# Mixture-of-experts stage of a diffusion layer: extra tokens' input products moved to pieces 13 and 14, with branch hints for TensorE

## The chip, the core and the metric

The kernel runs on one core of one Trainium2 chip. The metric is the device time of one execution in microseconds. Before the change it is 2446.74 us, the median of 3 runs (2444.03 to 2450.15).

## What is computed

One layer of a diffusion generator on 1024 latent tokens of width 1024: modulated RMSNorm, one projection, two kinds of attention, an output projection, and then a mixture of experts, which is what the change touches. Each token goes to 4 of 32 experts:

```python
def expert_block(args):
    xb, e = args
    hcat = xb @ w_in[e] + b_in[e]
    x_glu = jnp.minimum(hcat[:, :D_FF], SWIGLU_LIMIT)
    x_lin = jnp.clip(hcat[:, D_FF:], -SWIGLU_LIMIT, SWIGLU_LIMIT)
    act = x_glu * jax.nn.sigmoid(SWIGLU_ALPHA * x_glu) * (x_lin + 1)
    return act @ w_out[e] + b_out[e]
```

`w_in[e]` is 1024 x 2048 and `w_out[e]` 1024 x 1024, both float32. The outputs are weighted by the router's gates and summed per token. How many tokens an expert gets is known only at run time; on average it is 128.

## The kernel before, in words

The experts are `stage_e`. Its outer loop makes one pass for each expert e, plus one at the end. A pass has two halves: 16 input pieces of expert e (`in_mm`, half a row block of `w_in` each), then 8 output pieces of expert e - 1 (`out_mm`). A piece is six matmuls of 128 x 512 for TensorE: weights are split into a high and a low part and three products are summed (`mm3`, L87 to L89). The split of a piece is one copy on ScalarE (`wh`, L1131) and one subtraction on VectorE (`wl`, L1132). `split_ahead` keeps it up to 5 pieces ahead of TensorE, into 5 buffers of each (`NW`): after piece i of a pass stands the split of piece i + 5, so that behind input piece 14 comes the split of output piece 3, and behind input piece 15 that of output piece 4.

The first 128 tokens of an expert are handled with every piece. Tokens beyond 128 (up to 64 of them, in two units of 32) are the extra tokens: `left_in` and `left_out` compute their products on TensorE alone, inside a branch on the expert's count (`beyond`, L1159 for the first unit, L1161 for the second). The count is read into a register of TensorE's sequencer by `value_load` (L1168). Where the branch is not entered, TensorE's sequencer waits at it until TensorE is done, and signals in place of the products.

The order of all engines' work is written out by hand (`manual_schedule`): each engine runs its instructions in the order of the program text, and waits where its data are not there. Around the change it is, for a pass:

- after input piece 11 (`LB`): two PSUM banks for the extra tokens are cleared by ScalarE (`blank`, L1104);
- after input piece 15: `act_a(e)` clamps the 128 tokens' sums from PSUM, on VectorE (`ga` L1195, `ln` L1197) with ScalarE's activation between (L1196); then `left_in(e)`; then SP's loads of the next expert's `w_in`; then `act_l(e)`, which does for the extra tokens what `act_a` does: four clamps on VectorE (`gal` L1204 and `lnl` L1205 for each unit), then ScalarE's activation (L1206);
- after output pieces 1, 3 and 4: `columns(e + 1, 0..2)`, which transposes the next expert's gathered tokens on TensorE (L1119) and brings them back with a copy on ScalarE (L1122 or L1125) and, for the first two, a subtraction on VectorE (L1123). The third is for the extra tokens and has no subtraction;
- after output piece 5 (`KB`): one PSUM bank is cleared for the extra tokens' outputs; after output piece 7, `left_out(e - 1)`.

The PSUM banks of `columns`, `act_cols` (the transposes of the activations), `blank` and `left_in` all come from one tag, "r", which has two buffers taken in turn. In a pass nine tiles take them: three of `act_cols`, the two extra-token banks, three of `columns`, and the bank of the extra tokens' outputs. A tile can be written when all readers of the tile two turns before it are done.

```python
            def ring():
                return ps.tile([128, 512], F32, name="r", tag="r", bufs=2)
```

GpSimd issues the gathers of the tokens (L1060, L1068) and the scatters of the results (L1278, L1283); SP issues the weight loads.

Of the kernel before, what the change touches and what calls it, by code (L numbers as in the profile page):

```python
# [48 lines left out]
class K:  # L49
# [963 lines left out]
    def stage_e(self):  # L1013
        nc, I, tc = self.nc, self.I, self.tc
        ep = self.ep
        win, wout = I["w_in"], I["w_out"]
        NE = 32
        with ExitStack() as ctx:
# [4 lines left out]
            VAL = {}  # L1023
# [74 lines left out]
            def ring():  # L1098
                return ps.tile([128, 512], F32, name="r", tag="r", bufs=2)

            def blank():

                p = ring()
                nc.scalar.activation(p, zero.to_broadcast([128, 512]), AF.Copy)  # L1104
                return p
# [48 lines left out]
                    self.mm3(H[e][:, 1024 * h + 512 * b:1024 * h + 512 * b + 512], xh[:, k, :], xlo[:, k, :],  # L1154
                             wh[:, c], wl[:, c], False, k == 7)

            def beyond(e, unit):

                with tc.If(VAL[e] > 128):  # L1159
                    unit(0)  # L1160
                    with tc.If(VAL[e] > 160):  # L1161
                        unit(1)

            def left_in(e):

                xc = XT[e][2]
                ls = L[e]
                VAL[e] = nc.tensor.value_load(self.cnt[0:1, e:e + 1], min_val=0, max_val=1024)  # L1168

                def unit(u):  # L1170
                    for f in range(4):
                        o = ls[u][32 * f:32 * f + 32, :]
                        for g in range(2):
                            c = 1024 * g + 256 * f
                            q, c = divmod(c, 1536)
                            nc.tensor.matmul(o[:, 256 * g:256 * g + 256], sel(e, q, 32).bitcast(F32),
                                             self.bias[:, c:c + 256].bitcast(F32), start=g == 0, stop=False,
                                             tile_position=(0, 32 * f))
                    for k in range(8):
                        j, h = divmod(k, 2)  # L1180
                        for f in range(4):
                            w = RAW_IN[e][k].rearrange("p (g c) -> p g c", g=2)[:, :, 256 * f:256 * f + 256]
                            nc.tensor.matmul(ls[u][32 * f:32 * f + 32, :],
                                             xc[:, 2 * u + h, 32 * j:32 * j + 32], w,
                                             start=False, stop=k == 7, tile_position=(0, 32 * f))

                beyond(e, unit)

            A, AL = {}, {}
            COLS, KB, ACI, RI, LB, KAB = (1, 3, 4), 5, (3, 5, 7), 1, 11, 6  # L1190

            def act_a(e):
                gm = sp.tile([128, D], F32, name="ga", tag="ga", bufs=1)
# [6 lines left out]
            def act_l(e):  # L1200
                gm = sp.tile([128, 2, 256], F32, name="gal", tag="gal", bufs=1)
                ln = sp.tile([128, 2, 256], F32, name="lnl", tag="lnl", bufs=1)
                for u in range(2):
                    nc.vector.tensor_scalar(gm[:, u], L[e][u][:, :256], 7.0, None, op0=OP.min)  # L1204
                    nc.vector.tensor_scalar(ln[:, u], L[e][u][:, 256:], 7.0, -7.0, op0=OP.min, op1=OP.max)  # L1205
                nc.scalar.activation(gm, gm, AF.Gelu_apprx_sigmoid)  # L1206
                AL[e] = [gm, ln]
# [7 lines left out]
            def act_cols(e, g):  # L1215
                gm, gl = A[e][0], AL[e][0]
                if g == 0:
                    x = self.ap.tile([128, 16, 128], F32R, name="at", tag="kSa" if e < NE - 1 else "Q0")
                    ACT[e] = (x[:, 0:8], x[:, 8:16],
                              sp.tile([128, 4, 128], F32, name="ac", tag="ac", bufs=1))  # L1220
                ah, al, ac = ACT[e]
                p = ring()
                for i in range(4):
                    src = gm[:, 512 * g + 128 * i:512 * g + 128 * i + 128] if g < 2 else \
                        gl[:, i // 2, 128 * (i % 2):128 * (i % 2) + 128]
                    nc.tensor.transpose(p[:, 128 * i:128 * i + 128], src, self.ident)
                p3 = p.rearrange("p (k q) -> p k q", k=4)
                if g < 2:
                    nc.scalar.activation(ah[:, 4 * g:4 * g + 4], p3, AF.Copy)
                    nc.vector.tensor_sub(al[:, 4 * g:4 * g + 4], p3, ah[:, 4 * g:4 * g + 4].bitcast(F32))  # L1230
                else:
                    nc.scalar.activation(ac, p3, AF.Copy)
                    A.pop(e)
# [13 lines left out]
            def left_out(e):  # L1247
                ac = ACT[e][2]
                p = Y[e][2]

                def unit(u):
                    for j in range(4):
                        nc.tensor.matmul(p[32 * j:32 * j + 32, 256 * u:256 * u + 256],
                                         sel(e, 1, 32).bitcast(F32),
                                         self.bias[:, 512 + 256 * j:768 + 256 * j].bitcast(F32),
                                         start=True, stop=False, tile_position=(0, 32 * j))
                    for k in range(8):
                        jj, h = divmod(k, 2)
                        for j in range(4):
                            nc.tensor.matmul(p[32 * j:32 * j + 32, 256 * u:256 * u + 256],  # L1260
                                             ac[:, 2 * u + h, 32 * jj:32 * jj + 32],
                                             RAW_OUT[e][k // 2][:, 1024 * (k % 2) + 256 * j:1024 * (k % 2) + 256 * j + 256],
                                             start=False, stop=k == 7, tile_position=(0, 32 * j))

                beyond(e, unit)

            def result(e):
                y0, y1, yl = Y.pop(e)
# [52 lines left out]
            for e in range(NE + 1):  # L1321
                if 0 < e < NE - 1:
                    gather(e + 1)
                for i in range(16 if e < NE else 0):
                    in_mm(e, i)
                    if e > 0 or i < 13:
                        split_ahead(1)
                    else:
                        done[1] += 1
                    if i == RI and e > 1:  # L1330
                        result(e - 2)
                    if i in ACI and e > 0:
                        act_cols(e - 1, ACI.index(i))
                    if i == 0 and e == 0:
                        LLS = left_lists()
                    if i == 2 and e == 0:
                        left_lists2(*LLS)
                        gather_left(0)
                        load_out(0, range(2, 4), nc.gpsimd)
                    if i in (9, 10) and e == 0:  # L1340
                        columns(1, i - 9)
                    if i == 11 and e == 0:
                        columns(0, 2)
                        gather_left(1)
                    if i == LB:
                        L[e] = [blank(), blank()]
                if e == NE:
                    result(e - 2)
                if e < NE:
                    act_a(e)  # L1350
                    left_in(e)
                if e + 1 < NE:
                    load_in(e + 1, range(8) if e else range(2, 8))
                if e == NE - 1:
                    load_out(e)
                if e == 0:
                    load_out(0, range(2))
                    act_l(0)
                    split_ahead()
                    columns(1, 2)  # L1360
                elif e < NE:
                    act_l(e)
                for k in range(8 if e > 0 else 0):
                    out_mm(e - 1, k)
                    split_ahead(1)
                    if e < NE:
                        if k in COLS and e + 1 < NE:
                            columns(e + 1, COLS.index(k))
                        if k == (KAB if e < NE - 1 else 3):
                            act_b(e)  # L1370
                        if e == NE - 1 and k in (5, 6, 7):
                            act_cols(e, (5, 6, 7).index(k))
                    if k == KB:
                        Y[e - 1].append(blank())
                if e == 0:
                    act_b(e)
                if e > 0:
                    left_out(e - 1)
                    if e < NE:
                        if e < NE - 1:  # L1380
                            load_out(e)
                        split_ahead()
# [168 lines left out]
```

## Time and profile before

| | |
|---|---|
| median of 3 runs | 2446.74 us |
| the profiled execution | 2445.95 us |
| its span, first to last instruction | 2444.2 us |
| experts' stage (weights of the first to the last) | about 937 to 2405 us |
| TensorE busy | 2275.3 us, 93% |
| VectorE busy | 1938.9 us, 79% |
| ScalarE busy | 1505.0 us, 62% |

PE is TensorE's matmuls, PEld its weight loads, PEq its sequencer, DVE is VectorE, ACT ScalarE, POOL GpSimd, SP SyncE. Busy times are unions of the recorded instructions; a matmul is drawn from its start to a modelled end, so that neighbours overlap. An instruction is named by its line in the kernel and by the tiles that it writes and reads (`out<-in`).

### The profile page before, as it was taken

The numbers are of one execution on the slowest core, as the hardware profiler recorded it, in microseconds if no ns is written. First come the engines' busy times: TensorE is split into PE (matmuls) and PEld (weight loads), VectorE is DVE, ScalarE is ACT, GpSimd is POOL, SyncE is SP. The second block draws the span as 40 slices with busy tenths as digits, with TensorE's granted clock in tenths as the row PEclk, the third lists the DMA queues.
The fourth block names the chain that finished last, engine by engine and source line by source line (L and its number), as shares of the span: only waits on it lengthen the run. The fifth ranks groups of instructions, "written<-read, shape, count | busy, mean of one in ns | idle before, by whom it ended". The sixth has DMA issues, their size and how long they took to land. (4 is left out here: it accounts for less than half of the span.)

```text
span 2444.2 us, 36800 instructions
## 1 busy us (share of the span) xinstructions
PE 2275.3 (93%) x13516; PEld 1760.8 (72%) x13516; DVE 1938.9 (79%) x3051; ACT 1505.0 (62%) x2285; POOL 549.3 (22%) x699
## 2 busy tenths in 40 slices
PE   6999999999999997989999999999999999999993
PEld 3787777787888775767667777767767777777762
DVE  5897087777998677988768898778878978887884
ACT  4321077777888324767656776666767766766762
POOL 2402100000344433122112222112212212222211
PEclk9999999999999997999999999999999999999996
DMA  7546141111110646889778898879779779787875
GB/s 266 182 142 198 48 141 36 35 27 44 30 24 18 231 162 241 326 339 330 263 265 334 306 350 316 292 266 370 279 279 384 285 296 355 281 321 299 311 272 173
DMA packets 133890, 557.00 MB, mean 228 GB/s; under 512 B 18720, under 2 KB 29632, under 8 KB 100880
## 3 DMA queue, kind: packets, MB, share of 16 engines
q1 hardware_dynamic: 103472, 476.21, 51.0%
q0 software_dynamic: 30176, 77.43, 11.4%
q8 instruction: 169, 2.77, 0.5%
q14 instruction: 73, 0.60, 0.1%
HBM read 495.04 MB, written 50.14 MB: 223 GB/s over the span
## 5 line engine op out<-in xcount | busy, mean ns | idle before, releaser
L1131 ACT ACTIVATE wh<-rin 128x1024 fp32r<-128x1024 f32 x520 | 550.3, 1060 | 251.4 <-PE H L89 218.8
L1132 DVE TENSOR_TENSOR wl<-rin,wh 128x1024 fp32r<-128x1024 f32 x520 | 619.4, 1219 | 102.2 <-ACT wh L1131 100.8
L87 PE MATMUL H<-wh,xt 128*128 128x512 f32 x1024 | 414.1, 404 | 0.6 <-issue 0.5
L88 PE MATMUL H<-wl,xt 128*128 128x512 f32 x1024 | 405.5, 396 | 0.6 <-DVE wl L1132 0.6
L89 PE MATMUL H<-wh,xt 128*128 128x512 f32 x1024 | 405.2, 396 | 0.0
L1132 DVE TENSOR_TENSOR wl<-rout,wh 128x1024 fp32r<-128x1024 f32 x248 | 296.5, 1222 | 88.4 <-ACT wh L1131 84.6
L1131 ACT ACTIVATE wh<-rout 128x1024 fp32r<-128x1024 f32 x248 | 256.7, 1054 | 47.1 <-PE H L89 27.2
L89 PEld LDWEIGHTS H<-wh,xt 128*128 128x128 f32 x1024 | 193.5, 189 | 45.7
L87 PEld LDWEIGHTS H<-wh,xt 128*128 128x128 f32 x1024 | 193.9, 189 | 43.5 <-issue 1.4
L88 PEld LDWEIGHTS H<-wl,xt 128*128 128x128 f32 x1024 | 194.0, 189 | 42.7 <-DVE wl L1132 1.0
L87 PE MATMUL y<-wh,at 128*128 128x512 f32 x512 | 210.8, 412 | 0.0
L88 PE MATMUL y<-wl,at 128*128 128x512 f32 x512 | 203.2, 397 | 0.5 <-DVE wl L1132 0.5
L89 PE MATMUL y<-wh,at 128*128 128x512 f32 x512 | 203.4, 397 | 0.0
L1060 POOL DMA_INDIRECT xg<-h2d,im x31 | 33.5, 1081 | 658.8 <-PE r L1119 658.2
L622 ACT ACTIVATE PT<-T 128x512 f32<-128x512 f32 (+1 forms) x256 | 140.8, 577 | 54.4 <-PE T L621 51.9
L1283 POOL DMA_INDIRECT acc<-ol,il x64 | 151.3, 2364 | 17.0 <-DVE wl L1132 15.2
L621 PE MATMUL T<-ident,P 128*128 128x128 f32 x960 | 149.6, 279 | 3.3 <-DVE m L547 2.7
L557 ACT ACTIVATE P<-S,m 128x1024 f32<-128x1024 f32 x128 | 142.9, 1117 | 13.8 <-DVE m L545 7.2
L1278 POOL DMA_INDIRECT acc<-o,im x32 | 51.7, 1615 | 409.0 <-DVE o L1272 377.0
L88 PE MATMUL g<-wl,hh 128*128 128x512 f32 (+1 forms) x368 | 138.0, 375 | 4.1 <-POOL wl L232 4.1
L87 PE MATMUL g<-wh,hh 128*128 128x512 f32 (+1 forms) x368 | 139.1, 378 | 1.1 <-ACT wh L231 0.6
L89 PE MATMUL g<-wh,xl 128*128 128x512 f32 (+1 forms) x368 | 137.3, 373 | 0.0
(338 smaller groups left out, 4376.4 us busy)
## 6 DMA issues: line engine op xcount, KB each, us to landing
rin<-in_w_in SPq DMA_DIRECT2D x252, 1024.0 KB
rout<-in_w_out SPq DMA_DIRECT2D x122, 1024.0 KB
ld<-in_w_ada SPq DMA_DIRECT2D x48, 512.0 KB
wr<-in_w_qkv SPq DMA_DIRECT2D x32, 256.0 KB
Q<-Q SPq DMA_DIRECT2D x32, 256.0 KB
xl<-in_x SPq DMA_DIRECT2D x8, 512.0 KB
xr<-in_x SPq DMA_DIRECT2D x8, 512.0 KB
acc<-x POOLq DMA_DIRECT2D x8, 512.0 KB, 5.5
```

What stands on the lines that cost most here:

```text
L87: nc.tensor.matmul(p, ah, bh, start=start, stop=False)
L88: nc.tensor.matmul(p, ah, bl, start=False, stop=False)
L89: nc.tensor.matmul(p, al, bh, start=False, stop=stop)
L557: nc.scalar.activation(parts[k][0], parts[k][1], AF.Exp, bias=m, scale=0.125, accum_out=l2[:, k:k + 1])
L621: nc.tensor.transpose(p[:, k, :], P[:, 128 * j:128 * j + 128], self.ident)
L622: nc.scalar.activation(PT[u - 1][:, 4 * g:4 * g + len(w), :], p[:, :len(w)], AF.Copy)
L1060: nc.gpsimd.indirect_dma_start(out=xg, out_offset=None, in_=self.h2d[:, :], in_offset=bass.IndirectOffsetOnAxis(ap=self.im[:, e:e + 1], ax ...
L1131: nc.scalar.activation(h, src, AF.Copy)
L1132: nc.vector.tensor_tensor(l, src, h.bitcast(F32), op=OP.subtract)
L1278: sc = [nc.gpsimd.indirect_dma_start(out=self.acc[:, :], out_offset=bass.IndirectOffsetOnAxis(ap=self.im[:, e:e + 1], axis=0), in_=o, in_o ...
L1283: i = nc.gpsimd.indirect_dma_start(out=self.acc.rearrange("t (j d) -> (t j) d", j=4), out_offset=bass.IndirectOffsetOnAxis(ap=self.il[:, u ...
```

## The change

`left_in(e)` moves, for all experts but the first, from behind input piece 15 to behind input piece 13 (`LI`), and `act_l(e)` from behind `act_a(e)` to behind input piece 14. `value_load` moves from `left_in` to a new function, `hint`, which is called behind input piece 11 (`HI`) for the branch of `left_in` and behind output piece 5 (`HK`) for that of `left_out`. It reads the count if that has not been done, and places a branch hint in TensorE's instruction stream: the sequencer is told by the register whether the labelled branch will be entered. The inner branch (second unit) gets none.

```diff
+            def hint(e, what):
+
+                if e not in VAL:
+                    VAL[e] = nc.tensor.value_load(self.cnt[0:1, e:e + 1], min_val=0, max_val=1024)
+                tc.mark_branch_hint_location(f"{what}{e}", hint=VAL[e] > 128, engines=[mybir.EngineType.PE])
+
-            def beyond(e, unit):
+            def beyond(e, unit, what):
 
-                with tc.If(VAL[e] > 128):
+                with tc.If(VAL[e] > 128, label=f"{what}{e}"):
                     unit(0)
                     with tc.If(VAL[e] > 160):
                         unit(1)
...
-                VAL[e] = nc.tensor.value_load(self.cnt[0:1, e:e + 1], min_val=0, max_val=1024)
...
-            COLS, KB, ACI, RI, LB, KAB = (1, 3, 4), 5, (3, 5, 7), 1, 11, 6
+            COLS, KB, ACI, RI, LB, LI, KAB, HI, HK = (1, 3, 4), 5, (3, 5, 7), 1, 11, 13, 6, 11, 5
...
                     if i == LB:
                         L[e] = [blank(), blank()]
+                    if i == HI:
+                        hint(e, "in")
+                    if i == LI and e > 0:
+                        left_in(e)
+                    if i == LI + 1 and e > 0:
+                        act_l(e)
                 if e == NE:
                     result(e - 2)
                 if e < NE:
                     act_a(e)
-                    left_in(e)
+                    if e == 0:
+                        left_in(0)
...
                     act_l(0)
                     split_ahead()
                     columns(1, 2)
-                elif e < NE:
-                    act_l(e)
                 for k in range(8 if e > 0 else 0):
                     out_mm(e - 1, k)
                     split_ahead(1)
...
+                    if k == HK:
+                        hint(e - 1, "out")
                     if k == KB:
                         Y[e - 1].append(blank())
```

## Rows read from the trace of the kernel before

**Rows 1.** The page, part 1: busy us (share of the span) and instructions.

```profile
PE 2275.3 (93%) x13516; PEld 1760.8 (72%) x13516; DVE 1938.9 (79%) x3051; ACT 1505.0 (62%) x2285; POOL 549.3 (22%) x699
```

**Rows 2.** Busy time by stretch: PE, PEld, DVE, ACT, POOL, clock, DMA share, GB/s.

```profile
1400.00:1500.00 100.00, 95.89 (x480) 72.54 (x478) 90.33 (x94) 73.39 (x83) 23.67 (x17) 1.00 0.86 316
```

**Rows 3.** PE's waits, 990 to 2400 us: total us, times, longest us.

```profile
PE r L1119 <- issue: 26.2, 15, 1.8
PE H L1148 <- PEq L1159: 9.3, 5, 3.2
...
PE y L1239 <- PEq L1161: 5.9, 13, 0.6
PE y L1239 <- PEq L1159: 3.9, 2, 2.4
```

**Rows 4.** Timeline of DVE in expert 9's pass: start us, us, instruction, [idle before].

```profile
1368.14 4.85 DVE L1132 TENSOR_TENSOR wl<-rout,wh 128x1024 fp32r<-128x1024 f32 x4 [0.76 <-ACT wh L1131]
1372.91 1.22 DVE L1195 TENSOR_SCALAR ga<-H 128x1024 f32<-128x1024 f32 x1
...
1375.50 0.41 DVE L1205 TENSOR_SCALAR lnl<-r 128x256 f32<-128x256 f32 x1
1375.83 0.41 DVE L1204 TENSOR_SCALAR gal<-r 128x256 f32<-128x256 f32 x1
...
1377.89 2.36 DVE L1132 TENSOR_TENSOR wl<-rout,wh 128x1024 fp32r<-128x1024 f32 x2 [1.32 <-ACT wh L1131]
1380.17 0.69 DVE L1123 TENSOR_TENSOR xt<-r,xt 128x512 fp32r<-128x512 f32 x1
```

**Rows 5.** Timeline of TensorE in the same pass.

```profile
1370.00 0.40 PE L88 MATMUL H<-wl,xt 128*128 128x512 f32 x1
...
1370.23 0.40 PE L89 MATMUL H<-wh,xt 128*128 128x512 f32 x1
...
1370.78 0.70 PE L1239 MATMUL y<-bias,selm 128*128 128x512 f32 x2
...
1373.87 0.40 PE L89 MATMUL y<-wh,at 128*128 128x512 f32 x1
...
1376.02 0.63 PE L1119 MATMUL r<-ident,xg 128*128 128x128 f32 x4 [1.75 <-issue]
...
1380.91 0.56 PEld L1119 LDWEIGHTS r<-ident,xgl 128*128 128x128 f32 x4
```

**Rows 6.** Timeline of ACT in the same pass.

```profile
1369.26 1.06 ACT L1131 ACTIVATE wh<-rout 128x1024 fp32r<-128x1024 f32 x1 [0.20 <-PE H L89]
...
1374.16 1.06 ACT L1196 ACTIVATE ga<-ga 128x1024 f32<-128x1024 f32 x1 [2.42 <-DVE ga L1195]
1376.28 0.63 ACT L1206 ACTIVATE gal<-gal 128x512 f32<-128x512 f32 x1 [1.07 <-DVE gal L1204]
1376.82 1.99 ACT L1131 ACTIVATE wh<-rout 128x1024 fp32r<-128x1024 f32 x2
```

**Rows 7.** Timelines of DVE and PEld in expert 12's pass, which has extra tokens.

```profile
1500.03 0.42 DVE L1204 TENSOR_SCALAR gal<-r 128x256 f32<-128x256 f32 x1 [3.31 <-PE r L1183]
...
1506.27 0.68 DVE L1123 TENSOR_TENSOR xt<-r,xt 128x512 fp32r<-128x512 f32 x1
...
1508.63 0.59 PEld L1119 LDWEIGHTS r<-ident,xgl 128*128 128x128 f32 x4
```

**Rows 8.** TensorE's sequencer at L1159 and L1168: ns min/median/max, first and last start.

```profile
L1159 PEldq COMPARE_BRANCH  x64: 70/344/6846, 965.6 to 2399.5; - x64
...
L1168 PEldq TENSOR_LOAD <-cnt x32: 297/304/491, 964.7 to 2362.0; - x32
```

**Rows 9.** Busy time and granted clock by stretch, columns as in rows 2.

```profile
1056.16:1059.57 3.41, 2.97 (x7) 2.42 (x8) 1.37 (x2) 0.00 (x0) 0.00 (x0) 0.50 1.01 399
1059.57:1080.00 20.43, 20.43 (x95) 16.60 (x95) 17.37 (x18) 15.90 (x18) 6.54 (x5) 1.00 0.85 294
...
1371.00:1376.02 5.02, 3.27 (x15) 2.34 (x14) 4.89 (x7) 1.79 (x2) 0.00 (x0) 1.00 0.81 259
```

More of the change, by code (lines that the diff above doesn't have):

```diff
@@ L1185, in unit @@
                                              start=False, stop=k == 7, tile_position=(0, 32 * f))
-                beyond(e, unit)
+                beyond(e, unit, "in")
             A, AL = {}, {}
-            COLS, KB, ACI, RI, LB, KAB = (1, 3, 4), 5, (3, 5, 7), 1, 11, 6
+            COLS, KB, ACI, RI, LB, LI, KAB, HI, HK = (1, 3, 4), 5, (3, 5, 7), 1, 11, 13, 6, 11, 5
             def act_a(e):
@@ L1263, in unit @@
                                              start=False, stop=k == 7, tile_position=(0, 32 * j))
-                beyond(e, unit)
+                beyond(e, unit, "out")
             def result(e):
```

## The prediction

> **What bounds the kernel now.** I read the page first: TensorE is busy 93% of the span, VectorE 79% [rows 1], and in a stretch from the middle of the experts TensorE has 95.9% of the time at the full clock, VectorE 90.3% [rows 2]. So the experts are TensorE's, with VectorE close behind. The list of TensorE's waits in that stage comes next [rows 3]. It waits for two things: ahead of the transposes of the next expert's tokens (L1119: 26.2 us, 15 times, up to 1.8 us each), and for its own sequencer behind the branches on the extra tokens (L1159 and L1161). The change aims at both.
>
> The first wait is read from three timelines of the pass of expert 9, which has no extra tokens. VectorE clamps the main results from 1372.91 and then the extra ones; it has read the first of the two extra banks at 1375.91 [rows 4], and then TensorE transposes, at 1376.02, 2.15 us after the matmul before it where 0.23 is usual, so 1.92 us are lost [rows 5]. The reason is the tag "r": two buffers, nine takers a pass in turn, and the first columns take the buffer of the first extra-token bank. The same turn order says what comes next: **the third columns (the extra tokens') take the buffer of the first columns**, which is free when VectorE has subtracted their low part (L1123). That subtraction ends at 1380.86 and the third columns' weight load starts at 1380.91 [rows 4, 5]. It is no wait yet, since TensorE arrives just then; but nothing is left between them.
>
> **The change, part by part.** The clock of the argument is the end of piece 14, about 1369.26, where ScalarE's next split starts [rows 6].
>
> *The clamps at piece 14.* They now stand, on VectorE and ScalarE, between the splits of output pieces 3 and 4. Both engines keep program order. Today: ScalarE's half of piece 3 at 1369.26, VectorE's half of piece 4 ending at 1372.99, then the main clamps; ScalarE waits for the first of them and applies its function at 1374.16; the extra function follows at 1376.28, piece 5 at 1376.82; VectorE's half of piece 5 at 1377.89; 2.97 us later the first columns' subtraction ends [rows 4, 6]. After the change, the steps by the same rows: the empty branch's drain of TensorE (0.32 us, from the 0.55 between the last matmul of H and the next one, where 0.23 is usual [rows 5]) now lies ahead of piece 14, so ScalarE's half of piece 3 is at 1369.58, VectorE's 1.07 later (as 1376.82 to 1377.89) at 1370.65, the first extra clamp 1.14 later (a split of 1.22 less 0.08 of overlap) at 1371.79, the third two steps of 0.33 later at 1372.45. ScalarE's extra function needs that one (0.45 behind it: 1372.90), and **piece 4's ScalarE half now queues behind it**, 0.54 later at 1373.44. VectorE's half is at 1374.51, the main clamp at 1375.65, the main function 1.25 later at 1376.90, piece 5 on ScalarE 0.94 later at 1377.84, on VectorE at 1378.91; the subtraction has ended 2.97 later, at 1381.88, and the third columns start at 1381.93. That is 1.02 us after today's 1380.91. The chain has gained a round trip between the two engines, and lost only the clamps' 1.4 us behind the main ones.
>
> *TensorE* meanwhile has the first columns without their wait, and would be at the third columns at 1380.91 - 1.92 = 1378.99. It stands there for 1381.93 - 1378.99 = 2.94 us. So a pass without extra tokens is 1.02 us longer, not 1.92 shorter.
>
> A pass with extra tokens is hit harder. Today its main clamps run while TensorE does the extra products (VectorE waits 3.31 us for them after its main clamps), and the first columns' subtraction ended at 1506.95, 1.68 us ahead of the third columns at 1508.63 [rows 7]: no stall. After the change the products come before piece 14, VectorE has only piece 3 to split until piece 14 ends, and from there the chain is the one above: 2.94 us of stall, all of it new. The thirteen starts of output products released by L1161 in rows 3 count these passes; of the 30 passes with columns, 17 remain without. Sum: 13 x 2.94 = 38.2, 17 x 1.02 = 17.3, and the last pass, which has no columns but the same chain ahead of its activation, 1.0: **+56.5 us**.
>
> *The hints.* A branch takes 0.07 us where it falls through and up to 6.85 where it jumps [rows 8]; TensorE's queue covers most. What sticks out is, in rows 3, 9.3 us before H and 3.9 before y, less about 0.16 of drain in each of the seven: 12.1 us. Of the two before y (2.2 and 1.4 net) the greater part stood in for the wait at the first columns, which the sum above has already: third columns came 1.8 us later than in a usual pass in the one, no later in the other. So the hints can save 8.5 + 1.8 = 10.3. The inner test (L1161) has no hint. I take the full 10.3, since the fetch starts two pieces of six matmuls (2.8 us) earlier and at most 3.2 stuck out; the lower end is nothing. The hint itself has no row; the nearest is the count's load, 0.30 us on the same sequencer. If the queue hides it, as it hid 57 of the 64 outer branches, it costs nothing; if it hid none, 64 x 0.3 = 19. I take nothing.
>
> *Moved at no cost:* the count's load (sequencer, behind queued matmuls; without that cover 32 x 0.3 = 10 us). The matmuls themselves are the same. The raw input tiles come free about two pieces sooner, so SP's loads of the next expert can start sooner; no TensorE row waits for a load. GpSimd's gathers wait for the second columns and have a pass of time.
>
> *The clock.* The longest wait before H, 3.2 us, ended at 1056.6; from 1056.16 on the granted clock was 0.50 (1.2 GHz) for 3.41 us, in which 7 matmuls ran, against about 16 at the next stretch's 95 in 20.43 us; over the 1.75 us stall of expert 9 it stayed 1.00, or 2.4 GHz [rows 9]. All four waits on a missed branch over 2.3 us, and the one of 3.2 in the last pass, were followed by such a stretch; none of the fifteen of 1.75 was. Each costs some 1.5 us: of the 9 matmuls that are missing two fall to the end of the wait, and 7 at 0.215 are 1.5. The new stall would show as 2.8 us of idle time (2.94 less 0.16 by which drawn matmuls overlap), nearest to those that were followed by one. Ends: none of 30, or all, 45 us. Five cases are few, so I take two thirds, 20 stretches: +30. The four stretches after missed branches go: -6.
>
> Forecast: 56.5 - 10.3 + 30 - 6 = **+70 us**. The profiled execution took 2445.95 us (span 2444.2 and 1.75 around it), 0.8 below the median of the runs, 2446.74. 2445.95 + 70 = 2516 us.
>
> **The rivals.**
>
> *The clock falls at every stall:* 45 instead of 30, 2531 us. For it: five of five long waits in the trace. Against: those five had nothing but the wait in common with the new place, and it must turn out so 30 times. [...]
>
> *The hints do nothing:* the fetch stays where it is, or the hint displaces the code that follows. Then neither 10.3 nor 6 is saved: 56.5 + 30, 2532 us; with all stalls slowing the clock, 2547. For it: the DMA engines were full where the longest one ended (share 1.01 in rows 9), and a hinted fetch uses the same engines. [...]
>
> *Faster:* the first columns' buffer is free in time. Place: the subtraction L1123. It decides if it ends by 1378.99, 2.9 us sooner than I work out, which takes ScalarE's half of piece 4 (and then 5) being issued ahead of the extra function. Then 15 stalls of 1.92, 12.1 of branches and 6 of clock go: 2399 us. For it: rows 3 show no wait at the third columns today. Against: rows 4 and 6 run in program order throughout.
>
> *A draw:* the two engines lose a round trip but the stall at the third columns is about 1 us on average: 2447 us.
>
> **How the numbers follow.** Forecast 0.47, clock at every stall 0.18, hints idle 0.20, faster 0.11, draw 0.04. The range starts from the forecast without a single clock stretch (56.5 - 10.3 - 6 = +40, so 2486) and reaches to the hints idle with all stalls slow, 2547; the faster case and the draw lie outside. 0.3% (7 us) is about what a measurement of this kernel can tell from no change. Faster 0.11, same 0.04, slower 0.85.
>
> **What would show it.** Right: no idle time at the first columns, about 2.8 us ahead of the third in 30 passes; ScalarE idle ahead of the extra function and piece 4 behind it; half-clock stretches all through the experts; no branch wait over 0.5 us at L1159. Wrong: third columns without idle time, or the stall at the first columns still there.

## The result and the profile after

| | before | after |
|---|---|---|
| median of 4 runs each, measured side by side | 2445.39 us (2442.62 to 2450.15) | 2534.41 us (2531.85 to 2544.11) |
| ratio, 95% interval | | 1.0367 (1.035 to 1.0384) |
| the profiled execution; its span | 2445.95; 2444.2 us | 2544.11; 2542.3 us |
| experts, first product of H to the last matmul | 1464.9 us | 1556.8 us |
| mean granted clock | 0.977 | 0.957 |

The change costs 89 us. The profiled execution of after is the longest of its four, 9.7 us above the median, and some 6 us of that lie ahead of the experts (their first product starts at 944.8 us, before at 938.5), so its sums are read within the stage: +91.9 us there.

The page, part 1, of the kernel after (columns as in [rows 1]):

```profile
PE 2321.5 (91%) x13516; PEld 1794.8 (71%) x13516; DVE 1939.0 (76%) x3051; ACT 1494.8 (59%) x2285; POOL 531.2 (21%) x699
```

The same matmuls keep TensorE busy 46 us longer, and still it has a smaller share of the span than in [rows 1]. So there are both more idle time and slower matmuls. The same stretch as in [rows 2], now of after:

```profile
1400.00:1500.00 100.00, 88.68 (x394) 70.08 (x393) 85.49 (x93) 69.36 (x80) 20.43 (x18) 0.97 0.89 332
```

TensorE has lost 7 points, VectorE 5: neither is the bound, they wait for each other. TensorE's waits, 990 to 2500 us, answer to [rows 3]; line numbers from L1159 on have moved by 5 or 6 (in the runs below, by as many lines more or less as their edits add or take out), so L1165 is the outer branch and L1167 the inner:

```profile
PE r L1119 <- DVE xt L1123: 82.1, 30, 2.8
PE H L1148 <- PEq L1165: 10.6, 8, 2.0
PE H L87 <- PEq L1167: 5.4, 12, 0.5
```

The 26.2 us of 15 waits at the columns have become 82.1 us of 30, and the releaser is VectorE's low part of the first columns. The waits behind the outer branch ahead of H have not gone, and are eight instead of five. Those behind the inner branch of the input half are the same (5.4 ahead of H now, 5.9 ahead of y before), and only those on the outer branch before y have gone.

Where the stall comes from is read from expert 9's pass, as in [rows 4 to 6]. First ScalarE:

```profile
1398.02 1.06 ACT L1131 ACTIVATE wh<-rout 128x1024 fp32r<-128x1024 f32 x1 [0.59 <-PE H L89]
1401.37 0.63 ACT L1211 ACTIVATE gal<-gal 128x512 f32<-128x512 f32 x1 [2.29 <-DVE gal L1209]
1401.90 1.04 ACT L1131 ACTIVATE wh<-rout 128x1024 fp32r<-128x1024 f32 x1
...
1405.37 1.06 ACT L1201 ACTIVATE ga<-ga 128x1024 f32<-128x1024 f32 x1 [2.43 <-DVE ga L1200]
1406.34 1.99 ACT L1131 ACTIVATE wh<-rout 128x1024 fp32r<-128x1024 f32 x2
```

ScalarE stands idle for 2.29 us ahead of the extra tokens' function, and the split of output piece 4 (1401.90) queues behind it. VectorE in the same pass:

```profile
1399.11 1.23 DVE L1132 TENSOR_TENSOR wl<-rout,wh 128x1024 fp32r<-128x1024 f32 x1 [0.24 <-ACT wh L1131]
1400.25 0.42 DVE L1209 TENSOR_SCALAR gal<-r 128x256 f32<-128x256 f32 x1
...
1400.92 0.42 DVE L1209 TENSOR_SCALAR gal<-r 128x256 f32<-128x256 f32 x1
...
1402.98 1.23 DVE L1132 TENSOR_TENSOR wl<-rout,wh 128x1024 fp32r<-128x1024 f32 x1 [1.31 <-ACT wh L1131]
1404.12 1.22 DVE L1200 TENSOR_SCALAR ga<-H 128x1024 f32<-128x1024 f32 x1
...
1407.41 2.36 DVE L1132 TENSOR_TENSOR wl<-rout,wh 128x1024 fp32r<-128x1024 f32 x2 [0.95 <-ACT wh L1131]
1409.69 0.69 DVE L1123 TENSOR_TENSOR xt<-r,xt 128x512 fp32r<-128x512 f32 x1
```

VectorE waits for ScalarE at 1402.98 because of that queueing, and once more at 1407.41; the subtraction that frees the buffer ends at 1410.38. TensorE:

```profile
1402.48 0.60 PE L1119 MATMUL r<-ident,xg 128*128 128x128 f32 x4
...
1407.31 0.40 PE L89 MATMUL y<-wh,at 128*128 128x512 f32 x1
1410.43 0.66 PE L1119 MATMUL r<-ident,xgl 128*128 128x128 f32 x4 [2.72 <-DVE xt L1123]
...
1412.24 0.63 PE L89 MATMUL y<-wh,at 128*128 128x512 f32 x1
...
1418.68 0.70 PE L1148 MATMUL H<-bias,selm 128*128 128x512 f32 x2 [1.86 <-PEq L1165]
```

The first columns (1402.48) no longer wait. The third ones start at 1410.43, 0.05 us after VectorE's subtraction and 3.12 us after the matmul before them, where 0.23 is usual: 2.89 us are lost. From 1411.85 on matmuls come 0.43 us apart instead of 0.23, up to 1415.23. The clock of that stretch:

```profile
1411.92:1415.33 3.41, 3.41 (x10) 2.64 (x9) 3.41 (x4) 2.24 (x4) 1.39 (x2) 0.51 1.02 418
```

This is half clock, as in the 0.50 row of [rows 9]. Seven steps from 1412.24 to 1415.23 are 0.427 us each, and a matmul of 512 columns in 0.427 us makes 1.2 columns a ns. The profile gives the clock as a share alone; the prediction's 1.2 and 2.4 GHz are an estimate, this rate and its double with one column taken for a clock. Twenty-five of the 30 stalls were followed, or in one case overlapped, by such a stretch. From 990 us on, the stage had 20.5 us at half clock before (5 stretches, one of them double), and has 95.6 us in 26 after (two double).

**The balance of the stage,** from the start of each matmul to that of the next. The gaps ahead of the third columns grew by 87.0 us, those ahead of the other columns shrank by 29.2. Around the branches 4 us went, 3.6 of them the waits before y (the drains of the skipped branches only moved with them). What is left of the 91.9, +38, lies between matmuls that follow one another without a wait, all of it in output pieces and the third columns' own transposes. It fits the clock: 75 us more at half speed are some 37 us lost.

### The profile page after: what moved, and what is told of

It is laid out like the page before. It is cut to its first block, busy times and chain, and to the rows that moved or that the text cites. A ratio compares the mean times of both kernels' runs of the same rounds, so it can differ in the third digit from the quotient of the medians.

```text
span 2542.3 us, 36928 instructions
## 1 busy us (share of the span) xinstructions
PE 2321.5 (91%) x13516; PEld 1794.8 (71%) x13516; DVE 1939.0 (76%) x3051; ACT 1494.8 (59%) x2285; POOL 531.2 (21%) x699
## 5 line engine op out<-in xcount | busy, mean ns | idle before, releaser
L87 PE MATMUL y<-wh,at 128*128 128x512 f32 x512 | 226.2, 442 | 0.6 <-ACT wh L1131 0.6
L88 PE MATMUL y<-wl,at 128*128 128x512 f32 x512 | 217.9, 426 | 0.8 <-DVE wl L1132 0.8
L89 PE MATMUL y<-wh,at 128*128 128x512 f32 x512 | 216.8, 423 | 0.0
```

What stands on the lines that cost most here:

```text
L87: nc.tensor.matmul(p, ah, bh, start=start, stop=False)
L88: nc.tensor.matmul(p, ah, bl, start=False, stop=False)
L89: nc.tensor.matmul(p, al, bh, start=False, stop=stop)
```

## The experiments

Each is set against the kernel before run on the same chip (median 2447 to 2449 us). "Third columns" and "first columns" are the two places of the stall; a gap's loss is its length less 0.23 us.

### The change without its hints (e1_no_hints)

```diff
-                tc.mark_branch_hint_location(f"{what}{e}", hint=VAL[e] > 128, engines=[mybir.EngineType.PE])
```

> The changed kernel without the hint instructions; the count's load stays behind input piece 11. Theory (the third columns wait for the first columns' subtraction): the 30 stalls at L1119 of about 2.9 us and some 25 half-clock stretches stay, so 2534 us plus what the hints saved, 0 to 12: 2534 to 2546 us. Rival (the hints themselves cost time, by displacing code that is needed next): the waits behind the branches before H, 10.6 us in the changed kernel, shrink, and the time falls below 2530 us.

Measured: 2527.81 us, ratio 1.0319 (1.0297 to 1.0341). Its waits:

```profile
PE r L1119 <- DVE xt L1123: 82.0, 30, 2.8
PE H L1148 <- PEq L1164: 8.2, 5, 2.9
```

The column stall is the change's to 0.1 us, so the hints have no part in it. The time is lower than the changed kernel's, not higher: as placed, the hints cost about half a per cent. The waits behind the outer branch are fewer without them.

### The hints alone (e2_hints_only)

Before's kernel with `hint` and the labels, behind input piece 13 and output piece 5, and nothing moved but the count's load, which `hint` brings with it:

```diff
-            COLS, KB, ACI, RI, LB, KAB = (1, 3, 4), 5, (3, 5, 7), 1, 11, 6
+            COLS, KB, ACI, RI, LB, LI, KAB, HI, HK = (1, 3, 4), 5, (3, 5, 7), 1, 11, 13, 6, 13, 5
```

> The kernel before with the hints alone, behind input piece 13 and output piece 5 (two pieces ahead of each branch); products and clamps stay where they were. Theory: no stall at the third columns, the 15 at the first columns stay; the hints save the waits before y (3.6 us) and up to 8.5 before H: 2433 to 2445 us. Rival (the hints cost time): over 2452 us.

Measured: 2447.87 us, ratio 1.0000 (0.9983 to 1.0017). Both expectations miss:

```profile
PE r L1119 <- issue: 29.8, 17, 1.9
PE H L1148 <- PEq L1165: 12.9, 6, 3.2
...
PE y L1244 <- PEq L1167: 5.9, 13, 0.6
```

The two waits before y (3.9 us in [rows 3]) have gone, and the two first-column stalls that they had covered came up in their place (17 against 15). Those before H stayed, as long as ever. Two pieces ahead, the hints brought no time here.

### Products early, clamps left (e3_products_only)

```diff
-                    if i == LI + 1 and e > 0:
-                        act_l(e)
...
+                elif e < NE:
+                    act_l(e)
```

> The changed kernel with the extra tokens' clamps and activation back behind those of the 128 tokens; their products stay behind input piece 13. Theory: it is the place of the clamps between the splits that makes the third columns late. With them back, the stall is at the first columns, 1.9 us, now in all 30 passes instead of 15, none at the third columns, and the clock stays at 1.00: 2445 + 15 x 1.9 = 2474, less up to 10 of hints: 2464 to 2476 us. Rival (the place of the products does it): as the changed kernel, over 2520 us.

Measured: 2506.13 us, ratio 1.0218 (1.0191 to 1.0245).

```profile
PE r L1119 <- issue: 63.6, 30, 2.1
PE H L1148 <- PEq L1165: 17.3, 8, 3.5
```

With the clamps back, the stall is at the first columns again and the third lose nothing, as expected: it is the clamps' place that moves it. It is in all 30 passes, since the extra products no longer cover it in 13 of them. Each gap is 2.52 us, a loss of 2.29: the 1.92 of [rows 5] and about the 0.32 of the drain that now lies ahead of the chain. The time is 30 us above the upper end of what was expected: the stalls lose 69 us, where 30 x 1.9 = 57 were expected, and the branch waits and the half-clock stretches (17; after 10 of the 30 stalls) came on top.

### Third columns one piece later (e4_third_late)

```diff
-            COLS, KB, ACI, RI, LB, LI, KAB, HI, HK = (1, 3, 4), 5, (3, 5, 7), 1, 11, 13, 6, 11, 5
+            COLS, KB, ACI, RI, LB, LI, KAB, HI, HK = (1, 3, 5), 5, (3, 5, 7), 1, 11, 13, 6, 11, 5
```

> The changed kernel with the third columns one output piece later (behind piece 5 instead of 4). Theory: they wait for a buffer that VectorE frees at a fixed time, so one piece of work ahead of them takes 1.4 us off each of the 30 stalls of 2.9 us, and with 1.5 us idle the clock stays at 1.00: 2534 - 30 x 1.4 - 25 x 1.5 = 2455 us (2445 to 2470). Rival (they wait for something of their own, issued relative to them): stalls and clock as in the changed kernel, 2534 us.

Measured: 2505.98 us, ratio 1.0221 (1.0195 to 1.0246).

```profile
PE H L1148 <- PEq L1165: 32.9, 8, 4.8
PE y L88 <- DVE wl L1132: 23.5, 31, 0.8
PE r L1119 <- DVE xt L1123: 9.3, 30, 0.3
```

The columns' loss falls to 0.48 us, but TensorE now reaches output piece 5 before its low part is split, and loses 0.95 there in every pass: 1.43 in all, half of the change's 2.89 and close to the 1.5 that was forecast. So the late chain shows in whatever TensorE needs of it next. By the medians the time is 51 us above the forecast all the same. In the profile the three groups of waits ahead of H (32.9, 8.1 and 4.1 us) are 29 us more than the changed kernel's 15.9, and the clock, which was to stay up, is at half speed for 61 us, 58 of them in or behind those waits. Why the waits behind the outer branch trebled is taken up below.

### The extra function behind the main one (e5_gate_late)

```diff
-                nc.scalar.activation(gm, gm, AF.Gelu_apprx_sigmoid)
...
+            def act_g(e):
+                gm = AL[e][0]
+                nc.scalar.activation(gm, gm, AF.Gelu_apprx_sigmoid)
```

`act_g` is called behind `act_a`, so that ScalarE's split of piece 4 no longer queues behind it.

> The changed kernel with one instruction moved: ScalarE's activation of the extra tokens stands behind that of the 128 tokens, so that ScalarE's half of output piece 4 no longer queues behind it; VectorE's extra clamps stay behind the split of output piece 3. Theory (a round trip between the two engines was added to the chain): the first columns' subtraction ends 0.9 us sooner, the stall at the third columns falls from 2.9 to 2.0 us in all 30 passes, and a wait of 1.85 us of idle time is mostly too short for the clock to fall: 2534 - 27 - 38 = 2469 us (2460 to 2490). Rival (it is the amount of VectorE's work ahead of the subtraction, which this does not change): stalls and time as in the changed kernel, 2525 to 2540 us.

Measured: 2495.92 us, ratio 1.0192 (1.0173 to 1.0212).

```profile
PE r L1119 <- DVE xt L1123: 55.7, 30, 1.9
```

A gap is 2.24 us, a loss of 2.01 where 2.0 were expected: the round trip between the engines is worth 0.9 us a pass. The time is 27 us above the expected one, with 12 of the 30 stalls still followed by half clock and 14.4 us of waits behind branches.

### First columns one piece sooner (e6_first_early)

```diff
-            COLS, KB, ACI, RI, LB, LI, KAB, HI, HK = (1, 3, 4), 5, (3, 5, 7), 1, 11, 13, 6, 11, 5
+            COLS, KB, ACI, RI, LB, LI, KAB, HI, HK = (0, 3, 4), 5, (3, 5, 7), 1, 11, 13, 6, 11, 5
```

> The changed kernel with the first columns one output piece earlier (behind piece 0 instead of 1), so that their subtraction comes one split earlier in VectorE's order. Theory (the third columns wait for the buffer that this subtraction frees): the stall there falls by one split, 1.14 us, from 2.9 to 1.75 us in all 30 passes, the clock stays up, 2534 - 34 - 38 = 2462 us (2452 to 2485). Rival (the third columns have a date of their own, set by the chain of clamps or by their gather): the stall stays at 2.9 us, 2525 to 2540 us.

Measured: 2475.89 us, ratio 1.0101 (1.0082 to 1.012), inside the expected range.

```profile
PE r L1119 <- DVE xt L1123: 41.8, 30, 1.4
```

One number of the order is changed, and the loss at the third columns falls to 1.56 us. No stall is followed by half clock any more; the stage has 4 such stretches. Against the changed kernel the stage is 64 us shorter: 40 of stall (30 x 1.33) and 38 between the matmuls of the output pieces, which is all that the clock had cost, less some 6 of longer waits behind branches and 5 at the other columns. It is the clearest run for the theory of the buffer's turn.

### Three edits together, no hints (e7_three_edits)

The hint instruction is left out as in e1, the first and third columns are moved, and the extra function stands behind output piece 0 and the split that follows it:

```diff
+            COLS, KB, ACI, RI, LB, LI, KAB, HI, HK = (0, 3, 5), 5, (3, 5, 7), 1, 11, 13, 6, 11, 5
...
+                    if k == 0 and e < NE:
+                        act_g(e)
```

> The changed kernel without hints, with the extra tokens' activation behind the split of output piece 5 and the columns behind output pieces 0, 3 and 5. Theory: the first columns' subtraction ends about 10.0 us after the end of input piece 14 and TensorE is at the third columns about 11.0 us after it, so no stall is left there or at the first columns: the kernel before less its 15 stalls of 1.92 us, with the waits behind the branches as before: 2445 - 29 = 2416 us (2405 to 2435). Rival (VectorE and ScalarE cannot keep up, and each stall that is taken away comes back at the next weight split): about the kernel before, 2440 to 2460 us.

Measured: 2448.92 us, ratio 1.0004 (0.9991 to 1.0016).

```profile
PE H L1148 <- PEq L1164: 13.3, 5, 4.1
PE H L1148 <- PEq L1166: 8.5, 11, 2.5
PE r L1260 <- ACT r L1104: 8.3, 12, 0.7
...
PE H L1148 <- issue: 4.8, 1, 4.8
```

No column waits, in first or third place, and yet the kernel is no faster than before. In the profile (the fastest execution of the twelve, 8 us below the median) the first columns' 23.8 us are given back: 10.7 in waits ahead of H, 3.2 ahead of the transposes of the activations, and 9.2 in a new wait, where the extra tokens' output products wait for their bank to be cleared by ScalarE (L1104). The 4.8 us stand behind a branch that took 0.36: the sequencer comes one weight load further and then issues nothing until 1.4 us after a packet of 16 KB of instructions, which fits code that is late behind the branch. The half clock is 20.5 us, as before. The expected 2416 was wrong; the rival had the number, though not through the weight splits that it named.

### The output hint six pieces ahead (e8_out_hint_early)

```diff
-            COLS, KB, ACI, RI, LB, LI, KAB, HI, HK = (1, 3, 4), 5, (3, 5, 7), 1, 11, 13, 6, 11, 5
+            COLS, KB, ACI, RI, LB, LI, KAB, HI, HK = (1, 3, 4), 5, (3, 5, 7), 1, 11, 13, 6, 11, 1
```

> The changed kernel with the hint for the branch behind output piece 7 placed behind output piece 1, ahead of the stall at the third columns, instead of behind piece 5: 4 pieces (5.6 us) and a stall sooner. If a hint starts the fetch and only came too late (it was 1.0 us ahead of the branch on the sequencer), the 10.6 us of waits at L1165 before H go to under 2 us: 2520 to 2527 us. If a hint does not start a fetch, or what it fetches is gone again when the branch comes, they stay at 9 to 12 us: 2530 to 2540 us.

Measured: 2528.09 us, ratio 1.0324 (1.0309 to 1.0339).

```profile
PE r L1119 <- DVE xt L1123: 82.1, 30, 2.8
...
PE H L1148 <- PEq L1165: 2.2, 3, 1.5
```

The time is just above the expected 2520 to 2527, and that of the kernel without hints (1.0319). Waits behind the output branch fall from 10.6 us to 2.2. The branch of expert 9's pass, the changed kernel's and then this one's (ns min/median/max, start):

```profile
L1165 PEldq COMPARE_BRANCH  x1: 6935/6935/6935, 1411.6 to 1411.6; - x1
```

```profile
L1165 PEldq COMPARE_BRANCH  x1: 373/373/373, 1405.7 to 1405.7; - x1
```

So a hint can bring the code, if it is early enough. The trace's DMA records show the fetch itself, a packet of 16 KB of instructions. In the changed kernel it starts 4.4 us after this branch does, takes 1.1 us, and the branch ends 1.5 us behind it; here it starts 5.1 us behind the hint and ends 4.3 us ahead of the branch. Of the 32 output branches eight take over 3 us in the changed kernel. Five of them take 0.4 us here, each with such a packet 3.6 to 5.1 us behind its hint; the other three still take 5.4 to 6.6 us, and theirs comes only behind the branch. Why the hint started no fetch there is open. On the sequencer the changed kernel's hint stands 0.95 to 1.0 us ahead of that branch, not the 2.8 that two pieces take on TensorE: the sequencer is held at the third columns with the stalled weight load, and once that is free it issues the rest in a burst (in expert 9's pass the load starts at 1410.43, the hint at 1410.6, the branch at 1411.6). Here it stands 10.3 us ahead.

### No stall and early hints (e9_no_stall_early_hints)

As e7, with hints on behind input piece 8 and output piece 0, and the second columns one piece sooner:

```diff
-            COLS, KB, ACI, RI, LB, LI, KAB, HI, HK = (1, 3, 4), 5, (3, 5, 7), 1, 11, 13, 6, 11, 5
+            COLS, KB, ACI, RI, LB, LI, KAB, HI, HK = (0, 2, 5), 5, (3, 5, 7), 1, 11, 13, 6, 8, 0
```

> The changed kernel with the extra tokens' activation behind the split of output piece 5, the columns behind output pieces 0, 2 and 5, and the hints early: behind input piece 8 and output piece 0. Theory: no stall at the columns (the subtraction that frees the second columns' bank is one split sooner than in the run with three edits, so that the bank of the extra tokens' outputs is cleared in time and its 8.3 us of waits at L1260 go), and with the fetch started at least 6 pieces ahead the waits behind the branches (13.3 and part of 8.5 us there) go: 2447 - 29 - 8 = 2410 us (2402 to 2425), faster than the kernel before by over 1%. Rival (VectorE's order has no room, stalls come back elsewhere): 2435 to 2450 us.

Measured: 2432.07 us, ratio 0.9925 (0.991 to 0.994): faster than both kernels.

```profile
PE H L1148 <- PEq L1165: 9.2, 7, 2.0
PE r L1261 <- ACT r L1104: 8.3, 12, 0.7
PE H L1148 <- PEq L1167: 7.4, 11, 2.5
```

The stretch of [rows 2], in this kernel:

```profile
1400.00:1500.00 100.00, 98.16 (x492) 74.04 (x492) 86.71 (x94) 69.71 (x82) 21.23 (x17) 1.00 0.89 336
```

TensorE has 98.2% of the time at the full clock, 95.9 before. The stage takes 1452.1 us, 12.8 less than before's. It is not the 2410 that was expected: the wait for the cleared bank (8.3) and 16.6 us behind branches are left.

### Before's kernel with early hints (e10_before_early_hints)

As e2, with the hints behind input piece 9 and output piece 1:

```diff
+            COLS, KB, ACI, RI, LB, LI, KAB, HI, HK = (1, 3, 4), 5, (3, 5, 7), 1, 11, 13, 6, 9, 1
```

> The kernel before with the hints alone, placed early: behind input piece 9 and output piece 1, six pieces ahead of each branch instead of two. If the lead of a hint on the sequencer is what decides, the waits behind the outer branches (8.5 before H, 3.6 before y in the kernel before) and their four half-clock stretches (6 us) go: 2447 - 10 to 18 = 2429 to 2437 us. If hints are worth nothing here, 2443 to 2450 us, as with the hints two pieces ahead.

Measured: 2444.94 us, ratio 0.9985 (0.9973 to 0.9996).

```profile
PE r L1119 <- issue: 30.0, 17, 2.0
PE H L1148 <- PEq L1165: 7.4, 3, 2.9
```

Early hints by themselves give 0.15%, 3.5 us by the medians, less than the 0.3% that one can well tell: three waits are left of the six in e2, and the first-column stalls that the missed branches before y had covered are there. The time is in the range that was given for hints worth nothing.

### The changed kernel once more (e11_changed_again)

> The changed kernel once more, beside the others of this call. It took 1.0367 of the kernel before, and without its hints 1.0319, on another occasion. If the hints as the change has them cost time (theory: they come 1.0 us ahead of the branch behind output piece 7 and start more fetches than were needed), this is again over 1.035; if the two are the same kernel in time, near 1.032.

Measured: 2537.55 us, ratio 1.0374 (1.0348 to 1.04). The columns' waits are 82.3 us, 30 times, those behind the outer branch 12.0 us, 7 times. The first measurement holds, and with it the distance to e1, whose interval ends at 1.0341. That the hints as placed cost some 10 us is shown; where is only partly seen. The branch waits are 2 to 4 us of it, and the hint's own records are short: a median of 35 ns (at most 53) and 38 ns for its register operation, 64 times each, 5 us in all on a sequencer that is mostly ahead. The branches themselves show more: of the 32 output branches five take over 3 us in each of the four kernels without hints (before, e1, e7, e12), and eight in each of the seven with that hint 1 to 2.2 us ahead (the changed kernel in both runs, e2 to e6). With the hint 6 to 10 us ahead it is three to five (e8, e9, e10). Why a late hint adds long branches is open.

### No stall, no hints (e12_no_stall_no_hints)

Against e9:

```diff
-                tc.mark_branch_hint_location(f"{what}{e}", hint=VAL[e] > 128, engines=[mybir.EngineType.PE])
```

> The fastest kernel so far (no stall at the columns, hints six to eight pieces ahead; 0.9925 of the kernel before) without its hints. If the early hints are what set it apart from the run with three edits (1.0004), this is near 1.000 (0.997 to 1.002), with waits behind the branches of 13 us or more in place of 9.2; if it is the columns' place (second columns behind piece 2 instead of 3), it stays at 0.990 to 0.995.

Measured: 2448.05 us, ratio 1.0002 (0.999 to 1.0014).

```profile
PE H L1148 <- PEq L1164: 14.1, 5, 4.8
...
PE H L1148 <- issue: 4.3, 1, 4.3
```

The second line is a wait as the one of 4.8 us in e7, at the same place. The hint instruction is the only difference to e9, and it is the whole of e9's gain; the second columns' place, which sets this run apart from e7 (1.0004), is worth nothing. The outer branches, first here and then in e9:

```profile
L1164 PEldq COMPARE_BRANCH  x64: 70/342/6802, 964.5 to 2403.1; - x64
```

```profile
L1165 PEldq COMPARE_BRANCH  x64: 73/360/4018, 963.2 to 2386.1; - x64
```

In both, the longest branch less the longest wait is 2.0 us (6.8 - 4.8, 4.0 - 2.0): that much queued work TensorE still has when its sequencer reaches the output branch, 8 matmuls. Before it was 3.7 (6.85 - 3.2; 15 matmuls), in e4 2.1 (9 matmuls). In the changed kernel it is 15 matmuls too and 3.5 us at the full clock (6.68 - 3.15 in e11); in expert 9's pass it is 5.1 (6.94 - 1.86), because the half clock behind the stall falls on them. So without the stall a missed branch costs 1.7 us more than before, and this is how the columns' 23.5 us were lost again in e12: +8.8 ahead of H, +9.1 ahead of the extra outputs' bank and some 11 elsewhere, most of it between matmuls of input pieces, where the clock was at half speed for 34 us (17 in e9), less the 3.6 of the waits before y; the stage is 2.9 us longer than before's. Why the queued work differs (the place of the third columns, at which the sequencer can be held, goes with it: piece 4 before, piece 5 in e4 and e12; but e6 has piece 4 and 2.4 us, 10 matmuls) isn't settled.

## Why the prediction was right, and where not

**The bound and the turn of the buffers: right.** The stall left the first columns and appeared at the third in all 30 passes, released by the subtraction that the prediction named.

**The chain of the clamps at piece 14: right, step for step.** The prediction's clock starts with ScalarE's half of piece 3 at 1369.58; in the profile after it starts at 1398.02, so 28.44 is added to each of its times:

| step | predicted + 28.44 | measured |
|---|---|---|
| third extra clamp, VectorE | 1400.89 | 1400.92 |
| extra function, ScalarE | 1401.34 | 1401.37 |
| piece 4, ScalarE's half | 1401.88 | 1401.90 |
| main clamp, VectorE | 1404.09 | 1404.12 |
| main function, ScalarE | 1405.34 | 1405.37 |
| piece 5, VectorE's half | 1407.35 | 1407.41 |
| first columns' subtraction ends | 1410.32 | 1410.38 |
| third columns | 1410.37 | 1410.43 |

The stall was 2.94 us on paper and 2.89 in the trace, in passes with and without extra tokens alike. Predicted from it was +56.5 us; measured are 87.0 - 29.2 = +57.8, all in the 30 passes with columns. The 1.0 of the last pass did not come: TensorE waits 3.2 us ahead of its transposes (L1226, now L1231), as before. e5 and e6 took 0.88 and 1.33 us out of it by the two ways that the chain allows, and e3 put it back to the first columns.

**The hints, -10.3 us: wrong.** This was the step "I take the full 10.3, since the fetch starts two pieces of six matmuls (2.8 us) earlier". The lead was counted on TensorE's matmuls, but the hint runs on the sequencer, which after the third columns covers two pieces in 1.0 us; 10.6 us of waits stayed, up to 2.0 each, where the prediction's own sign was none over 0.5. The rival "the hints do nothing" describes this: 2532 us, 2 below the median measured. It was the rival's first reason, that the fetch stays where it is: in the eight long output branches its packet starts 3.0 to 4.4 us behind the branch, in before's five 2.1 to 4.3. What the prediction put forward for this rival, that the DMA engines are full, is weakened by e8 and e9, where early hints worked at DMA shares of 0.91 and 0.89 (1400 to 1500 us). Its second reason, that the hint displaces the code that follows, is not excluded: eight long output branches stand against five. Of the 10.3 us only the 3.6 before y went, and not by the hints, since e1 does not have those waits either. Against the change without hints they cost some 10 us, where the prediction had nothing, within its upper end of 19. The outer branches took 344 ns in the median before [rows 8] and 372 after, and up to 6.9 us.

**The clock, +30 - 6 us: right in kind, too small.** Twenty of 30 stalls were taken to be followed by half clock, at 1.5 us each; it was 25 here, and 21 in e1 and e11. The 38 us over 21 more stretches (26 against 5) are 1.8 each: some are of double length, 6.83 us. A single one costs what was taken: in expert 9's pass 9 matmuls from 1411.85 to 1415.49 took 3.64 us for 2.10. The four old stretches behind missed branches did go, as the sum had it: in this profile none follows a branch; the waits that stayed there are 2.0 us at most (in e11 three are 2.9 to 3.2, and each is followed by one). So 25 new stretches stand against the 20 in the sum. The first rival had all 30 stalls followed by one; the trace shows 25.

**The sum.** By the balance of the stage: columns +57.8 for +56.5, branches -4 for -10.3, clock +38 for +24, together +92 for +70. The mechanism carried the forecast; the 22 us missing are 14 of clock, 6 of branches and 1 of the columns. By the medians of the runs, 2534.41 against 2516, 18 are missing. The rivals at 2531 and 2532 came nearer, and each has a part of what was missing.

## What to carry to other kernels

When a wait on a shared buffer is removed by moving its reader, look for who takes the buffer next in turn, and write the new order of every engine it passes through on paper; here that gave the new stall to 0.05 us. A stall's price is also what it does to the clock behind it (half speed behind 25 of 30 stalls here, some 38 us of the stage's 91.9), and what work it leaves in the queue for the next branch (2.0 to 3.7 us). A branch hint's lead is to be counted on the sequencer, from the last place that holds it: 1 us brought nothing, and 10 us shortened five of eight long branches.

## What the runs showed of the hardware

- Idle time of TensorE at the columns and the half clock behind it, by the length of the idle row: 2.7 to 2.8 us, 21 to 25 of 30 times; 2.1 us (e3), 10 of 30; 1.9 us (e5), 12 of 30; 1.75 us (before) and 1.4 us (e6), never. In e2 one of 17, of 1.94 us, was. The prediction had rows for the fourth and, behind branches, near the first.
- A branch that jumps can hold the sequencer for up to 6.9 us (7.2 in e3), and a packet of 16 KB of instructions ends 1.3 to 1.5 us before it does. With the hint 1.0 us ahead the eight long output branches took 5.5 to 6.9 us (the changed kernel), with 2.2 us 4.1 to 5.0 (e6); with 10.3 us (e8) five of the changed kernel's eight took 0.4, and three still 5.4 to 6.6.
- How much matmul work is queued when the sequencer reaches a branch differs by the order of the work, from 2.0 us (8 matmuls, e12) to 3.7 (15, before), so a missed branch of 6.8 us costs 4.8 us in one kernel and 3.2 in the other.
